# Two matmuls instead of three per block: the source's high and low part side by side in one 512-column matmul

## The chip, the core and the metric

The kernel runs on one core of a Trainium2 chip. The metric is device time in microseconds of one launch, the median of several runs. Beside the timed runs there is one execution with the hardware profiler; its span runs from the first to the last instruction.

## What is computed

A trunk of two transformer layers on 256 tokens with 1024 features, all in float32. Each layer is: half an FFN, an attention mixer, cross attention to 256 memory tokens, half an FFN. The mixer of the first layer joins differential and stick-breaking heads, that of the second is latent attention.

```python
def swiglu(h, w_gate, w_up, w_down):
    return (jax.nn.silu(h @ w_gate) * (h @ w_up)) @ w_down
...
    for layer in range(DEPTH):
        x = x + 0.5 * swiglu(rms_norm(x, ffn_norm[layer, 0]), ...)
        h = rms_norm(x, mix_norm[layer])
        x = x + mixer(h)            # ends in mixed @ w_out (layer 0), from_heads(o) @ w_o (layer 1)
        x = x + memory_cross_attention(rms_norm(x, xm_norm[layer]), rms_norm(mem, ...), ...)
        x = x + 0.5 * swiglu(rms_norm(x, ffn_norm[layer, 1]), ...)
```

The change concerns `@ w_down` (four times) and the output projections of the two mixers and the two cross attentions.

## The kernel before, in words

**Products from high and low parts.** Every operand of a large product is split into a high part (rounded to the matmul's type) and a low part, what the rounding left. A product of two such pairs is three matmuls: high x high, high x low, low x high (`mm3`, lines 268 to 272). Weights come from memory in chunks of up to 2048 columns. ACT casts a piece to `wh` (line 237), DVE subtracts to get `wl` (line 239); in attention phases GpSimd (POOL) takes the last 512 columns. Three buffers of `wh` and `wl` hold the chunks in flight, and SP's queue issues their transfers two chunks ahead.

**Layout.** The residual `x` lies feature-major, eight tiles of [128 features, 256 tokens]. In the down and output projections the weight block [128, 128] is the stationary operand and the source [128, 256 tokens] the moving one, so the result of an output tile needs 256 columns of a PSUM bank of 512. The sources (`slotr` in the trace) are slots of 512 columns; a slot holds two row blocks side by side, and high and low parts have slots of their own (`rpair`, line 469).

**FFN.** `ffn` makes 11 gate and 11 up products of two row blocks each and keeps the 22 split results in slots. Then `dp` runs over four pairs of output tiles; each pair takes two of the three `mm` banks, and for each of three weight chunks both tiles accumulate 8, 8 and 6 row blocks: 44 blocks a pair. PE's order is the program's.

**Output projections.** `out_g` does the same in the attention phases: 8 row blocks per tile after a mixer, 4 after cross attention. The first three tiles run as a group over the sources as they come, the other five one by one. There PE's order comes from a planner (`run`) that counts estimated times (`spend`, `drop`) and is fixed before the run. The order of the other engines' instructions is settled by the framework's scheduler.

**End of a tile.** `finish_dt` (line 481) adds the bank to `x` on DVE (line 484), splits the result times the next norm's gain into `xh` on ACT (line 462) and `xl` on DVE (line 463), squares it on ACT (line 496) and adds the squares on POOL (line 504). The next phase's first product reads the eight `xh`, `xl` pairs in turn, three matmuls each, and starts before the norm is known; the norm's sum and its spread over the partitions (line 526) are put in later.

Of the kernel before, what the change touches and what calls it, by code (L numbers as in the profile page):

```python
# [19 lines left out]
P = 128  # L20
# [10 lines left out]
# columns of the packed per-partition vectors  # L31
# [26 lines left out]
# estimates that settle the order of the tensor engine's work in the attention phases  # L58
# [92 lines left out]
def trunk_kernel(ctx, tc, wflat, xT_d, memT_d, gains_d, rows_d, cst_d, out_d):  # L151
# [35 lines left out]

    def alr():
        return alloc("r")
# [54 lines left out]
    def issue_part(i, h, n):  # L244
        """one of n parts of a chunk"""
# [21 lines left out]

    def mm3(out, a, b, first, last, **kw):
# [17 lines left out]
    # the tensor engine's clock rises while it works  # L286
# [10 lines left out]
    # chunk mask as a rank-one product: rows 0 and 64 hold it, the others are 0  # L297
# [15 lines left out]
    def setup():  # L313
# [12 lines left out]
        # rotary tables with the gains folded in  # L326
# [21 lines left out]
        # -(lambda) on every partition  # L348
# [69 lines left out]
    def run(first, tasks):  # L418
        """first: the first weight used"""
# [31 lines left out]
    def colsum(items, get):  # L451
        """items: lists of [128, 128] blocks; sums over partitions (and the list), tokens on partitions."""
# [7 lines left out]
    def split(hi, lo, src, g):  # L460
        """hi + lo = src * g (per partition)"""
# [7 lines left out]
    def rpair():  # L469
        return alr(), alr()  # L470
# [1078 lines left out]
```

## Time and profile before

| | us |
|---|---|
| median of 3 runs | 1130.59 (1129.61 to 1134.78) |
| span of the execution with the profile | 1131.1 |
| PE (TensorE) busy | 1104.2 |
| DVE busy | 783.8 |
| ACT busy | 653.3 |
| POOL busy | 214.5 |

Matmuls are pipelined: the length of one in the trace covers its whole way, so their pace is read from one start to the next. Each matmul has a weight load of its own (PEld), which runs beside the matmul before it. The stages follow each other in the span: first FFN to about 205 us, first mixer to 344, cross attention to 386, two FFNs to 576 and 765, latent mixer to 898, cross attention to 939, last FFN to the end.

### The profile page before, as it was taken

The numbers are of one execution on the slowest core, as the hardware profiler recorded it, in microseconds if no ns is written. First come the engines' busy times: TensorE is split into PE (matmuls) and PEld (weight loads), VectorE is DVE, ScalarE is ACT, GpSimd is POOL, SyncE is SP. The second block draws the span as 40 slices with busy tenths as digits, with TensorE's granted clock in tenths as the row PEclk, the third lists the DMA queues.
The fourth block names the chain that finished last, engine by engine and source line by source line (L and its number), as shares of the span: only waits on it lengthen the run. The fifth ranks groups of instructions, "written<-read, shape, count | busy, mean of one in ns | idle before, by whom it ended". The sixth has DMA issues, their size and how long they took to land.

```text
span 1131.1 us, 23384 instructions
## 1 busy us (share of the span) xinstructions
PE 1104.2 (98%) x9042; PEld 1084.4 (96%) x9042; DVE 783.8 (69%) x1864; ACT 653.3 (58%) x1765; POOL 214.5 (19%) x232
## 2 busy tenths in 40 slices
PE   7999999899999999999999999999979999999998
PEld 7999999899999999999999999999868999999998
DVE  6977656668876867676666767556688668676753
ACT  5755545677755755555555555556866566555542
POOL 4200001547244200000100000015861412000000
PEclk8999999999999999999999999999999999999999
DMA  6555555543445354545455555565342434555561
GB/s 232 218 192 183 180 193 187 187 150 119 143 150 174 114 188 169 192 175 200 170 186 189 185 187 178 176 197 187 113 131 66 153 134 147 203 182 192 177 207 65
DMA packets 49647, 191.39 MB, mean 169 GB/s; under 512 B 5632, under 2 KB 7296, under 8 KB 34432
## 3 DMA queue, kind: packets, MB, share of 16 engines
q1 hardware_dynamic: 49536, 189.89, 49.0%
q8 instruction: 71, 1.16, 0.4%
q14 instruction: 40, 0.33, 0.1%
HBM read 188.82 MB, written 1.05 MB: 168 GB/s over the span
## 4 chain that ended last, share of the span: by engine, by line
PE 85%; DVE 8%; issue 2%; ACT 2%; POOL 2%; DMA 0%; SPq 0%; DVEq 0%; POOLq 0%; ACTq 0%
PE mm L269 27%; PE mm L270 27%; PE mm L271 27%; DVE wl L239 3%; DVE xl L463 2%; PE t L723 1%; POOL sm L448 1%; ACT wh L237 1%; PE t L456 1%; DVE x L484 1%; POOL sl L448 0%; PE s L861 0%; PE o L1432 0%; PE s L1399 0%; ACT xh L462 0%
## 5 line engine op out<-in xcount | busy, mean ns | idle before, releaser
L237 ACT CAST wh<-wr 128x256 fp32r<-128x256 f32 (+1 forms) x1216 | 439.9, 433 | 341.8 <-PE mm L270 298.7
L239 DVE TENSOR_TENSOR wl<-wr,wh 128x256 fp32r<-128x256 f32 (+1 forms) x1171 | 482.6, 470 | 119.1 <-ACT wh L237 114.2
L270 PE MATMUL mm<-xl,wh 128*128 128x256 f32 x1584 | 447.7, 283 | 7.0 <-DVE xl L463 7.0
L269 PE MATMUL mm<-xh,wh 128*128 128x256 f32 x1584 | 448.7, 283 | 2.6 <-ACT wh L255 1.3
L271 PE MATMUL mm<-xh,wl 128*128 128x256 f32 x1584 | 446.4, 282 | 0.0
L270 PEld LDWEIGHTS mm<-xl,wh 128*128 128x128 f32 x1584 | 300.4, 190 | 9.3 <-DVE xl L463 9.1
L269 PEld LDWEIGHTS mm<-xh,wh 128*128 128x128 f32 x1584 | 300.5, 190 | 3.7 <-ACT wh L255 1.5
L271 PEld LDWEIGHTS mm<-xh,wl 128*128 128x128 f32 x1584 | 300.5, 190 | 0.2 <-DVE wl L256 0.2
L269 PE MATMUL mm<-slotr,wh 128*128 128x256 f32 x896 | 252.4, 282 | 0.0
L270 PE MATMUL mm<-slotr,wh 128*128 128x256 f32 x896 | 251.4, 281 | 0.0
L271 PE MATMUL mm<-slotr,wl 128*128 128x256 f32 x896 | 251.4, 281 | 0.0
L269 PEld LDWEIGHTS mm<-slotr,wh 128*128 128x128 f32 x896 | 168.9, 189 | 0.4 <-issue 0.3
L270 PEld LDWEIGHTS mm<-slotr,wh 128*128 128x128 f32 x896 | 168.9, 189 | 0.1
L271 PEld LDWEIGHTS mm<-slotr,wl 128*128 128x128 f32 x896 | 168.9, 188 | 0.0
L504 POOL TENSOR_TENSOR acc<-acc,sq 128x256 f32<-128x256 f32 x56 | 46.7, 833 | 529.5 <-ACT sq L496 523.8
L239 POOL TENSOR_TENSOR wl<-wr,wh 128x512 fp32r<-128x512 f32 x45 | 68.0, 1511 | 108.5 <-ACT wh L237 108.4
L671 DVE TENSOR_TENSOR slotf<-mm,rb 128x512 f32<-128x512 f32 x44 | 30.4, 690 | 79.1 <-PE mm L271 79.1
L663 DVE TENSOR_TENSOR slotf<-mm,rb 128x512 f32<-128x512 f32 x44 | 30.4, 690 | 37.4 <-PE mm L271 37.4
L269 PE MATMUL mm<-wh,slotr 128*128 128x256 f32 (+2 forms) x176 | 55.4, 315 | 0.0
L462 ACT ACTIVATE xh<-x,gains 128x256 fp32r<-128x256 f32 x64 | 32.0, 507 | 37.7 <-DVE x L484 35.2
L271 PE MATMUL mm<-wh,slotr 128*128 128x256 f32 (+2 forms) x176 | 53.3, 303 | 0.0
L270 PE MATMUL mm<-wl,slotr 128*128 128x256 f32 (+2 forms) x176 | 53.1, 302 | 0.0
(191 smaller groups left out, 1106.4 us busy)
## 6 DMA issues: line engine op xcount, KB each, us to landing
wr<-wflat SPq DMA_DIRECT2D x118, 1024.0 KB, 4.8
wr<-wflat SPq DMA_DIRECT2D x180, 256.0 KB, 4.0
wr<-wflat SPq DMA_DIRECT2D x16, 768.0 KB, 4.3
slotf<-memT SPq DMA_DIRECT2D x8, 256.0 KB, 6.0
x<-xT SPq DMA_DIRECT2D x4, 256.0 KB, 5.3
wr<-wflat SPq DMA_DIRECT2D x2, 512.0 KB, 8.1
out<-x SPq DMA_DIRECT2D x8, 128.0 KB, 3.7
cst<-cst SPq DMA_DIRECT2D x1, 256.0 KB, 8.1
```

What stands on the lines that cost most here:

```text
L237: A.copy(hi[:, a:b], raw[:, a:b])
L239: e.tensor_tensor(out=lo[:, a:b], in0=raw[:, a:b], in1=hi[:, a:b].bitcast(F32), op=ALU.subtract)
L269: PE.matmul(out, a[0], b[0], start=first, stop=False, **kw)
L270: PE.matmul(out, a[0], b[1], start=False, stop=False, **kw)
L271: PE.matmul(out, a[1], b[0], start=False, stop=last, **kw)
L448: G.tensor_tensor(out=y, in0=v, in1=mhalf[:, 0:n], op=ALU.pow)
L456: PE.matmul(ps[:, 2 * c:2 * c + 2], b, ones[:, 0:2], start=k == 0, stop=k == len(blocks) - 1)
L462: A.activation(hi, src, AF.Identity, scale=g)
L463: V.scalar_tensor_tensor(out=lo, in0=src, scalar=g, in1=hi.bitcast(F32), op0=ALU.mult, op1=ALU.subtract)
L504: G.tensor_tensor(out=st.acc, in0=st.acc, in1=sq, op=ALU.add)
L663: V.tensor_tensor(out=t.rearrange("p (a b) -> p a b", b=S), in0=pg.rearrange("p (a b) -> p a b", b=S), in1=rbb, op=ALU.mult)
L671: V.tensor_tensor(out=u.rearrange("p (a b) -> p a b", b=S), in0=pu.rearrange("p (a b) -> p a b", b=S), in1=rbb, op=ALU.mult)
```

## The change

Per block, `mm2` takes the place of `mm3` in the down and output projections. The source's high and low part now lie side by side in one slot of 1024 columns (`Pair`: two row blocks, each 256 columns high and 256 columns low). One matmul of 512 columns multiplies the high weights with both and fills the whole bank; one of 256 columns multiplies the low weights with the high part and accumulates onto the second half. `finish_dt` then adds the bank's two halves to `x` one after the other. Everything else that makes slots (memory tiles, latent pairs, stick-breaking sums) uses the same pairs and reads them in parts; the other products keep `mm3`. The planner counts 0.231 + 0.118 us for a block, and 1.2 for the release of a bank, instead of 0.327 and 0.8.

```diff
-            for key, n, dt in (("f", n32, F32), ("r", n32r, F32R)):
-                ar[key] = [pool.tile([P, 512], dt, name=nm("slot" + key)) for _ in range(n)]
+            for key, n, dt, w in (("f", n32, F32, 512), ("r", n32r // 2, F32R, 1024)):
+                ar[key] = [pool.tile([P, w], dt, name=nm("slot" + key)) for _ in range(n)]
...
+    def mm2(bank, w, src, first, last):
+        PE.matmul(bank[:, 0:512], w[0], src[2], start=first, stop=False)
+        PE.matmul(bank[:, S:512], w[1], src[0], start=False, stop=last)
+        spend(0.231 + 0.118)
...
-    def rpair():
-        return alr(), alr()
+    class Pair:
+        def __init__(self):
+            self.t = alloc("r")
+            self.v = self.t.rearrange("p (q h s) -> p q h s", h=2, s=S)
+            self.h, self.l = self.v[:, :, 0, :], self.v[:, :, 1, :]
+            self.blocks = [(self.v[:, q, 0, :], self.v[:, q, 1, :], self.t[:, q * 512:(q + 1) * 512])
+                           for q in range(2)]
...
     def finish_dt(dt, gc, ps=None, factor=1.0):
         xd = x[:, dt, :]
         if ps is not None:
-            V.scalar_tensor_tensor(out=xd, in0=ps, scalar=factor, in1=xd, op0=ALU.mult, op1=ALU.add)
+            for h in range(2):
+                V.scalar_tensor_tensor(out=xd, in0=ps[:, h * S:(h + 1) * S], scalar=factor, in1=xd,
+                                       op0=ALU.mult, op1=ALU.add)
...
     def out_g(keyf, nchunk, groups, gc):
...
-                mm3(pss[dt][:, 0:S], (w[0][:, k, j * P:(j + 1) * P], w[1][:, k, j * P:(j + 1) * P]),
+                mm2(pss[dt], (w[0][:, k, j * P:(j + 1) * P], w[1][:, k, j * P:(j + 1) * P]),
                     src[i], g == 0 and i == 0, g == len(groups) - 1 and i == len(rows_) - 1)
...
-                finish_dt(dt, gc, ps[:, 0:S])
-                drop(ps, 0.8)
+                finish_dt(dt, gc, ps)
+                drop(ps, 1.2)
...
     def ffn(l, j, gc, need_rb):
...
-            hh, hl = rpair()
-            split1(hh, hl, u)
+            h = Pair()
+            split1(h.h, h.l, u.rearrange("p (a b) -> p a b", b=S))
...
-                        mm3(pss[q][:, 0:S], (w[0][:, i, q * P:(q + 1) * P], w[1][:, i, q * P:(q + 1) * P]),
+                        mm2(pss[q], (w[0][:, i, q * P:(q + 1) * P], w[1][:, i, q * P:(q + 1) * P]),
                             hs[k], k == 0, k == FT - 1)
```

**PE, start of the first FFN's down projection.** Each row is a matmul: output bank, source slot and weight buffer, then the size of the output. Before:

```order
L269 MATMUL mm_1869<-slotr_109,wh_1727 128x256
L270 MATMUL mm_1869<-slotr_110,wh_1727 128x256
L271 MATMUL mm_1869<-slotr_109,wl_1726 128x256
L269 MATMUL mm_1869<-slotr_109,wh_1727 128x256
L270 MATMUL mm_1869<-slotr_110,wh_1727 128x256
L271 MATMUL mm_1869<-slotr_109,wl_1726 128x256
```

And now, the same two blocks and half of the next:

```order
L268 MATMUL mm_1858<-slotr_109,wh_1716 128x512
L269 MATMUL mm_1858<-slotr_109,wl_1715 128x256
L268 MATMUL mm_1858<-slotr_109,wh_1716 128x512
L269 MATMUL mm_1858<-slotr_109,wl_1715 128x256
L268 MATMUL mm_1858<-slotr_110,wh_1716 128x512
```

High and low part are in one slot, and a block has two rows. PE's order is the same in all else, but for two output blocks in the latent mixer that stand behind a group of four transposes instead of ahead of it.

**DVE, end of the first FFN** (tiles 6 and 7 of the last pair; `wl_...` is the next phase's weight chunk; line 496 of the changed kernel is the addition, 467 the low part, 236 the weight subtraction). Before:

```order
L484 SCALAR_TENSOR_TENSOR x<-mm_2486,x 128x256 [waits PE_49]
L463 SCALAR_TENSOR_TENSOR xl_2668<-x,gains,xh_2667 128x256 [waits Activation_49]
L484 SCALAR_TENSOR_TENSOR x<-mm_2487,x 128x256 [waits PE_49]
L239 TENSOR_TENSOR wl_2738<-wr_2737,wh_2739 128x512 [waits DMAHW2_49,Activation_49]
L239 TENSOR_TENSOR wl_2738<-wr_2737,wh_2739 128x512 [waits DMAHW3_49,Activation_49]
L463 SCALAR_TENSOR_TENSOR xl_2676<-x,gains,xh_2675 128x256 [waits Activation_49]
L239 TENSOR_TENSOR wl_2738<-wr_2737,wh_2739 128x512 [waits DMAHW4_49,Activation_49]
```

Now:

```order
L496 SCALAR_TENSOR_TENSOR x<-mm_2349,x 128x256 [waits PE_49]
L496 SCALAR_TENSOR_TENSOR x<-mm_2349,x 128x256 [waits DVE_49]
L467 SCALAR_TENSOR_TENSOR xl_2488<-x,gains,xh_2487 128x256 [waits Activation_49]
L496 SCALAR_TENSOR_TENSOR x<-mm_2350,x 128x256 [waits PE_49]
L236 TENSOR_TENSOR wl_2549<-wr_2548,wh_2550 128x512 [waits DMAHW2_49,Activation_49]
L496 SCALAR_TENSOR_TENSOR x<-mm_2350,x 128x256 [waits DVE_49]
L236 TENSOR_TENSOR wl_2549<-wr_2548,wh_2550 128x512 [waits DMAHW3_49,Activation_49]
L236 TENSOR_TENSOR wl_2549<-wr_2548,wh_2550 128x512 [waits DMAHW4_49,Activation_49]
L467 SCALAR_TENSOR_TENSOR xl_2497<-x,gains,xh_2496 128x256 [waits Activation_49]
```

A second addition, which waits for the first, and a third weight subtraction stand between tile 7's matmuls and its low part.

**DVE, end of the first cross attention** (tiles 4 to 7; the weight chunk is the next FFN's). Before:

```order
L463 SCALAR_TENSOR_TENSOR xl_4946<-x,gains,xh_4945 128x256 [waits Activation_49]
L484 SCALAR_TENSOR_TENSOR x<-mm_4952,x 128x256 [waits PE_49]
L484 SCALAR_TENSOR_TENSOR x<-mm_4973,x 128x256 [waits PE_49]
L463 SCALAR_TENSOR_TENSOR xl_4967<-x,gains,xh_4966 128x256 [waits Activation_49]
L484 SCALAR_TENSOR_TENSOR x<-mm_4994,x 128x256 [waits PE_49]
L463 SCALAR_TENSOR_TENSOR xl_4988<-x,gains,xh_4987 128x256 [waits Activation_49]
L239 TENSOR_TENSOR wl_5053<-wr_5052,wh_5054 128x256 [waits DMAHW0_49,Activation_49]
L463 SCALAR_TENSOR_TENSOR xl_5009<-x,gains,xh_5008 128x256 [waits Activation_49]
```

Now:

```order
L496 SCALAR_TENSOR_TENSOR x<-mm_4692,x 128x256 [waits PE_49]
L496 SCALAR_TENSOR_TENSOR x<-mm_4674,x 128x256 [waits DVE_49]
L496 SCALAR_TENSOR_TENSOR x<-mm_4692,x 128x256 [waits DVE_49]
L496 SCALAR_TENSOR_TENSOR x<-mm_4710,x 128x256 [waits PE_49]
L467 SCALAR_TENSOR_TENSOR xl_4686<-x,gains,xh_4685 128x256 [waits Activation_49]
L496 SCALAR_TENSOR_TENSOR x<-mm_4710,x 128x256 [waits DVE_49]
L467 SCALAR_TENSOR_TENSOR xl_4704<-x,gains,xh_4703 128x256 [waits Activation_49]
L496 SCALAR_TENSOR_TENSOR x<-mm_4728,x 128x256 [waits PE_49]
L467 SCALAR_TENSOR_TENSOR xl_4722<-x,gains,xh_4721 128x256 [waits Activation_49]
L496 SCALAR_TENSOR_TENSOR x<-mm_4728,x 128x256 [waits DVE_49]
L236 TENSOR_TENSOR wl_4773<-wr_4772,wh_4774 128x256 [waits DMAHW0_49]
L236 TENSOR_TENSOR wl_4773<-wr_4772,wh_4774 128x256 [waits Activation_49] x2
```

Behind these rows stands the last low part: three weight subtractions ahead of it instead of one. The chunk before (`wl_4655`, seven rows) now stands ahead of tile 4's first addition.

## Rows read from the trace of the kernel before

**Rows 1.** The page: busy time of the engines, the last chain's shares.
```profile
PE 1104.2 (98%) x9042; PEld 1084.4 (96%) x9042; DVE 783.8 (69%) x1864; ACT 653.3 (58%) x1765; POOL 214.5 (19%) x232
...
PE 85%; DVE 8%; issue 2%; ACT 2%; POOL 2%; DMA 0%; SPq 0%; DVEq 0%; POOLq 0%; ACTq 0%
PE mm L269 27%; PE mm L270 27%; PE mm L271 27%; DVE wl L239 3%; DVE xl L463 2%; PE t L723 1%; POOL sm L448 1%; ACT wh L237 1%; PE t L456 1%; DVE x L484 1%; POOL sl L448 0%; PE s L861 0%; PE o L1432 0%; PE s L1399 0%; ACT xh L462 0%
```

**Rows 2.** The page's groups: count, busy us, mean ns | idle before, releaser.
```profile
L269 PE MATMUL mm<-slotr,wh 128*128 128x256 f32 x896 | 252.4, 282 | 0.0
...
L484 DVE SCALAR_TENSOR_TENSOR x<-mm,x 128x256 f32<-128x256 f32 x64 | 26.6, 418 | 23.6 <-PE mm L271 23.6
```

**Rows 3.** Timeline, DVE, first down projection: start, length (us), instruction, [idle before].
```profile
156.74 0.42 DVE L484 SCALAR_TENSOR_TENSOR x<-mm,x 128x256 f32<-128x256 f32 x1
...
172.41 0.42 DVE L484 SCALAR_TENSOR_TENSOR x<-mm,x 128x256 f32<-128x256 f32 x1
```

**Rows 4.** Timeline, PE, latent mixer: 256 columns, then 512.
```profile
790.05 0.28 PE L269 MATMUL mm<-wh,slotr 128*128 128x256 f32 x1
...
791.85 0.28 PE L269 MATMUL mm<-wh,slotr 128*128 128x256 f32 x1
...
792.22 0.39 PE L269 MATMUL mm<-wh,slotr 128*128 128x512 f32 x1
792.45 0.39 PE L270 MATMUL mm<-wl,slotr 128*128 128x512 f32 x1
792.68 0.40 PE L271 MATMUL mm<-wh,slotr 128*128 128x512 f32 x1
792.92 0.39 PE L269 MATMUL mm<-wh,slotr 128*128 128x512 f32 x1
```

**Rows 5.** Timeline, PE, latent mixer: 384 columns, the first and the nineteenth.
```profile
809.78 0.34 PE L269 MATMUL mm<-wh,slotr 128*128 128x384 f32 x1
...
812.96 0.34 PE L269 MATMUL mm<-wh,slotr 128*128 128x384 f32 x1
```

**Rows 6.** Waits of PE: who waited <- for whom: us in total, times, longest.
```profile
PE mm L270 <- DVE xl L463: 7.0, 7, 1.4
PE t L526 <- issue: 2.9, 1, 2.9
```

**Rows 7.** Timeline, DVE and PE, ends of the first FFN and the second (last row).
```profile
204.95 0.42 DVE L484 SCALAR_TENSOR_TENSOR x<-mm,x 128x256 f32<-128x256 f32 x1 [0.36 <-PE mm L271]
205.53 1.29 DVE L239 TENSOR_TENSOR wl<-wr,wh 128x512 fp32r<-128x512 f32 x2 [0.15 <-ACT wh L237]
206.75 0.48 DVE L463 SCALAR_TENSOR_TENSOR xl<-x,gains,xh 128x256 fp32r<-128x256 f32 x1
...
207.37 0.31 PE L270 MATMUL mm<-xl,wh 128*128 128x256 f32 x1
...
219.60 0.76 PE L526 MATMUL t<-slotf,ones 128*128 128x256 f32 x2 [2.85 <-issue]
...
578.17 0.47 DVE L463 SCALAR_TENSOR_TENSOR xl<-x,gains,xh 128x256 fp32r<-128x256 f32 x1
```

**Rows 8.** Timeline, DVE and PE, start of the FFN after cross attention.
```profile
389.19 0.94 DVE L463 SCALAR_TENSOR_TENSOR xl<-x,gains,xh 128x256 fp32r<-128x256 f32 x1
...
390.19 0.38 PE L270 MATMUL mm<-xl,wh 128*128 128x256 f32 x1 [0.83 <-DVE xl L463]
```

**Rows 9.** Timeline, PE, start of cross attention; busy us by stretch before two boundaries.
```profile
348.33 0.38 PE L270 MATMUL mm<-xl,wh 128*128 128x256 f32 x1 [0.94 <-DVE xl L463]
...
331.00:346.00 15.00, 15.00 (x129) 15.00 (x128) 13.65 (x22) 10.86 (x26) 10.03 (x9) 1.00 0.44 141
379.00:391.00 12.00, 11.00 (x90) 10.61 (x90) 11.57 (x26) 10.14 (x31) 5.96 (x7) 1.00 0.40 148
```

The columns of the last two are: length; PE, PEld, DVE, ACT and POOL busy (and their instructions); granted clock, share of the DMA engines, GB/s.

**Rows 10.** Timeline, DVE and SP's queue, end of the run.
```profile
1128.01 0.42 DVE L484 SCALAR_TENSOR_TENSOR x<-mm,x 128x256 f32<-128x256 f32 x1 [1.69 <-PE mm L271]
1128.46 0.33 SPq L486 DMA_DIRECT2D out<-x  x1
```

More of the change, by code (lines that the diff above doesn't have):

```diff
@@ L594, in tm_g @@
             for k in range(KT):
-                a = tuple(z[:, t * P:(t + 1) * P] for z in xg[k])
+                a = tuple(z[:, t * P:(t + 1) * P] for z in xg[k][:2])
                 mm3(ps[:, t * S:(t + 1) * S], a, (w[0][:, k, :], w[1][:, k, :]), k == 0, k == KT - 1)
@@ L673, in ffn @@
             V.tensor_tensor(out=u, in0=u, in1=s, op=ALU.mult)
-            hh, hl = rpair()
-            split1(hh, hl, u)
+            h = Pair()
+            split1(h.h, h.l, u.rearrange("p (a b) -> p a b", b=S))
             rel(u, s)
-            tiles += [hh, hl]
-            for q in range(2):
-                hs.append((hh[:, q * S:(q + 1) * S], hl[:, q * S:(q + 1) * S]))
+            tiles.append(h.t)
+            hs += h.blocks
         begin_phase()
@@ L742, in mem_gain @@
             nc.sync.dma_start(raw.rearrange("p (a b) -> p a b", b=S), memT_d[:, 2 * q:2 * q + 2, :])
-            h, lo = rpair()
-            memstate["tiles"] = memstate.get("tiles", []) + [h, lo]
+            h = Pair()
+            memstate["tiles"] = memstate.get("tiles", []) + [h.t]
             for j in range(2):
-                sl_ = slice(j * S, (j + 1) * S)
-                split(h[:, sl_], lo[:, sl_], raw[:, sl_], gcol(G_MEM + l * KT + 2 * q + j))
-                xm.append((h[:, sl_], lo[:, sl_]))
+                split(h.blocks[j][0], h.blocks[j][1], raw[:, j * S:(j + 1) * S], gcol(G_MEM + l * KT + 2 * q + j))
+            xm += h.blocks
             if first:
@@ L883, in attend @@
             rel(*pT)
-            hh, hl = rpair()
-            split1(hh, hl, po)
-            tiles.extend([hh, hl])
-            srcs[hp] += [(hh[:, j * S:(j + 1) * S], hl[:, j * S:(j + 1) * S]) for j in range(2)]
+            h = Pair()
+            split1(h.h, h.l, po.rearrange("p (a b) -> p a b", b=S))
+            tiles.append(h.t)
+            srcs[hp] += h.blocks
             drop(po, 1.3)
@@ L920, in mixer_ab, with add_src @@
         raw = {}
-        def add_src(i, hh, hl):
-            tiles.extend([hh, hl])
-            srcs[i] += [(hh[:, j * S:(j + 1) * S], hl[:, j * S:(j + 1) * S]) for j in range(2)]
+        def add_src(i, h):
+            tiles.append(h.t)
+            srcs[i] += h.blocks
         def products():
@@ L1028, in stick @@
                 rel(e)
-                hh, hl = rpair()
-                split1(hh[:, 0:384], hl[:, 0:384], sp[:, 0:384])
-                sps.append((sp, hh, hl))
-            for i, (z, (sp, hh, hl)) in enumerate(zip(zs, sps)):
+                pr = Pair().t
+                split1(pr[:, 0:384], pr[:, 512:896], sp[:, 0:384])
+                sps.append((sp, pr))
+            for i, (z, (sp, pr)) in enumerate(zip(zs, sps)):
                 yield dict(lat=EST_AB['st2'] if i else EST_AB['st1'])
-                for h_ in (hh, hl):
-                    PE.matmul(z[:, 0:384], ntri, h_[:, 0:384], start=False, stop=False, skip_group_check=True)
+                for o in (0, 512):
+                    PE.matmul(z[:, 0:384], ntri, pr[:, o:o + 384], start=False, stop=False, skip_group_check=True)
                 PE.matmul(z[:, P:S], nones, sp[:, S:384], start=False, stop=True, skip_group_check=True)
@@ L1156, in turn_o @@
             pt = transpose4([oa[t][:, (2 * g + j) * P:(2 * g + j + 1) * P] for j in range(2) for t in range(2)])
-            hh, hl = rpair()
-            split(hh, hl, pt, gsub)
-            add_src(2 + g, hh, hl)
+            h = Pair()
+            split(h.h, h.l, pt.rearrange("p (a b) -> p a b", b=S), gsub)
+            add_src(2 + g, h)
             drop(pt, 1.4)
@@ L1180, in latent @@
             pairs, sqs = lat[key]
-            hh, hl = rpair()
+            h = Pair()
             for j in range(2):
-                sl_ = slice(j * S, (j + 1) * S)
-                split(hh[:, sl_], hl[:, sl_], ps[:, sl_], gcol(gc0 + j))
-                pairs.append((hh[:, sl_], hl[:, sl_]))
-            lat_tiles.extend([hh, hl])
+                split(h.blocks[j][0], h.blocks[j][1], ps[:, j * S:(j + 1) * S], gcol(gc0 + j))
+            pairs += h.blocks
+            lat_tiles.append(h.t)
             sq = al()
@@ L1436, in attend @@
             rel(*pT)
-            hh, hl = rpair()
-            split1(hh, hl, po)
-            tiles.extend([hh, hl])
-            srcs[n] += [(hh[:, j * S:(j + 1) * S], hl[:, j * S:(j + 1) * S]) for j in range(2)]
+            h = Pair()
+            split1(h.h, h.l, po.rearrange("p (a b) -> p a b", b=S))
+            tiles.append(h.t)
+            srcs[n] += h.blocks
             drop(po, 1.3)
```

16 lines of the change are left out of this document (7 added, 9 removed).

## The prediction

> **What bounds the kernel now.** I read the page first: TensorE is busy for 98% of the span, and the chain that ended last lies on it for 85%, 81% in the three lines of the three-matmul helper [rows 1]. So a shorter stream of matmuls shortens the time wherever the engine does not wait. Of that stream the change touches the 896 blocks that write an output tile from a slot: 704 in the four down projections (4 x 8 tiles x 22 row blocks), 192 in the four output projections [rows 2].
>
> The length of one matmul in the trace (281 ns) holds its way through the array; what counts is start to start. The DVE's additions give it without any counting of matmuls: between the first additions of two neighbouring pairs of tiles lie 2 x 22 x 3 = 132 matmuls, and they are 172.41 - 156.74 = 15.67 us apart, 118.7 ns each [rows 3]. TensorE's granted clock is 1.00 in the stretches that I read [rows 9], so 2.4 GHz, at which 256 columns alone are 106.7 ns. Something is on top, and how it divides between "per matmul" and "per column" is all that this change can win.
>
> The trace of before has wide matmuls, in the key and value products of the latent mixer, right behind narrow ones of the same kind. Fifteen of 256 columns take 791.85 - 790.05 = 1.80 us, 120.0 ns each; three of 512 take 792.92 - 792.22 = 0.70 us, 233.3 ns each [rows 4]. Eighteen of 384 take 3.18 us, 176.7 ns [rows 5]. The three widths lie on one line: 6.7 ns per matmul and 0.443 ns per column (384 x 0.443 + 6.7 = 176.7). Two narrow ones in one wide one thus save 6.7 ns.
>
> Then I read the waits: PE lost 7.0 us in seven waits for the low part of the normed residual, and 2.9 us in one wait of the matmul that spreads the norm [rows 6]. The seven lie at the start and at the ends of stages, where the last addition, the high part and the low part follow each other and the next stage's eighth block needs the result. That is the place where this change adds work.
>
> **The change part by part.** *Matmuls.* Per block three of 256 columns become one of 512 and one of 256. In the 704 down blocks that is 704 x 6.7 ns, **-4.7 us**, all on the path, since PE does not wait inside the down stages. The 192 blocks of the output projections would give 1.3 us more, but these end behind the DVE (below), so I count 0 there. Bounds for all 896: nothing, if a wide one follows the slowest distance of the wide rows (0.24 us, two narrow ones are 0.237), and 6.6 us at the fastest distance (0.23 us, 7.4 ns a block). I stay with the mean of three. A loss is unlikely, since that mean is below two narrow ones in the same row.
>
> *Weight loads.* One in three goes. No PE wait on them stands inside the down stages, so 0.
>
> *A second addition per tile.* 64 more of 0.42 us on DVE [rows 2], and the order shows that each waits for the DVE's own first addition. Inside a stage this is covered: a pair of tiles takes 15.67 us and the additions 0.84 more; the third bank and the 22 blocks ahead of the next need cover the later release. At a stage's end it is not. Start of the first addition: the wide matmul of the last block ends one narrow matmul earlier, 0.12 us gained.
>
> *End of the run.* The last addition starts at 1128.01 and the output's transfer is issued at 1128.46 [rows 10]. One more addition, 0.42, with some 0.05 for the wait, less 0.12: **+0.35**.
>
> *FFN into an attention stage* (twice). Before, two weight subtractions (1.29 together) stand between the last addition and the low part, which is ready at 206.75 + 0.48 = 207.23; the matmul that reads it starts at 207.37 without a wait [rows 7], so the slack is 0.1 at most. In the new order the second addition (0.42) and a third subtraction (0.65) stand there too: 1.07 later, less 0.12 and the slack, a wait of some 0.85. At the first of the two PE soon waits 2.85 us for the norm's spread [rows 7], which hangs on the DVE's work on freshly loaded memory tiles, not on PE; the new wait disappears in it: 0. At the second, into the latent mixer, no such wait follows within 30 us: **+0.9**. Bounds 0 and 1.0 for each.
>
> *Mixer into cross attention* (twice). PE already waits 0.94 us for the low part, and the DVE is busy 13.65 of the 15 us before [rows 9]. Five tiles finish there one by one: five additions are 2.1 us against 1.35 us of idle time. Bounds: 0.35 (own addition only) and 2.1 (none of the idle time is usable, since it is spent waiting for casts). I take 1.0: the overflow of 0.75 and a little of the idle time. **+2.0**.
>
> *Cross attention into FFN* (twice). PE waits 0.83 us [rows 8], the DVE is busy 11.57 of 12 us [rows 9]. Bounds 0.35 and 2.1 - 0.43 = 1.7. I take 0.6, towards the lower end: in the new order seven weight subtractions stand ahead of the fifth tile's addition, so that the tail holds additions, low parts and three subtractions, where before the low part was itself stretched to 0.94 us beside them. **+1.2**.
>
> *FFN into FFN* (once): the low part starts at 578.17 [rows 7] and PE does not wait. A third subtraction and the second addition move it, but the first low part of the pair is moved too. 0 to 0.6, **+0.2**.
>
> *The rest.* The casts and subtractions into slots write two strided halves, same count and elements; 0. The larger slots are handed out in the same turn. The planner's new figures move two output blocks in the latent mixer past one group of transposes: 0.
>
> Sum: -4.7 + 0.35 + 0.9 + 2.0 + 1.2 + 0.2 = **-0.05 us**. The execution with the profile had a span of 1131.1 us; the median of the three runs lies 0.5 us below it. 1131.1 - 0.05 - 0.5 = 1130.6 us (rounded).
>
> **The rivals.** *The ends are covered* (0.20). If the stage ends cost their lower bounds (0 + 0 + 0.7 + 0.7 + 0 + 0.35 = 1.75) and the output projections keep their gain (6.7 ns x 896 = 6.0), the sum is -4.25: 1126.4. For it: the low part at the cross boundary was stretched by other work, which can fall elsewhere. Against it: the DVE has hardly any idle time there [rows 9].
>
> *The DVE becomes the bound at the ends of the output projections* (0.13), slower than before. One mechanism: five late tiles x one addition, none of the idle time usable: 2 x 2.1 + 2 x 1.7 = 7.6 instead of 3.2, so +4.35: 1135.0. It decides from the point where these additions delay the low part by over 0.8 us at each of the four boundaries; with the 1.45 us of the other ends the matmuls' 4.7 us are eaten then. For it speaks that DVE waits in order, so an addition that waits for PE holds the subtractions behind it.
>
> *The overhead goes with the columns* (0.15), so the wide matmul is worth two narrow ones and the change wins nothing on PE. For it: one of three wide ones took 0.24 us to the next (792.68 to 792.92), two narrow ones 0.24 [rows 4]; and the three widths were read in another stage, where the moving operand is a weight. Against it: all three widths fit one line. The ends alone would give +4.65: 1135.2 us, and half of the saving 1132.9.
>
> The Trainium skill speaks for a part of this: TensorE: Matmul & The Clock Gate, "Back-to-back issue gap", gives the distance of warm matmuls as N / 2.4 ns plus about 2.5 ns. The trace disagrees, with 118.7 and 233.3 ns where that would be 109 and 216. By that split the down blocks would save 1.8 us, and the time would come to 1133.5 us.
>
> **How the numbers follow.** My case, gain and ends cancel, has 0.52, with its own range of 1128 to 1133. About 0.5% (5.65 us) is what a measurement of this kernel can tell from no change. Faster by more (under 1124.9) needs the covered ends and the highest gain: 0.05. Slower by more (over 1136.2) needs the DVE case or that of the columns with the upper bounds of the other ends: 0.09. Same: 0.86. The range of 8 in 10 reaches from the lower part of the covered case to the DVE case, 1125.5 to 1135.5.
>
> **What would show it.** Right: first additions of neighbouring pairs 15.67 - 44 x 0.0067 = 15.37 us apart in the first FFN; wide matmuls 231 to 233 ns apart from the next; at the boundary into the latent mixer a new PE wait of near 0.9 us for the low part, at the first boundary the same with a shorter wait of the norm's spread; waits near 2 us into cross attention and 1.4 us into the FFN. Wrong: pairs still 15.67 us apart (no gain); PE waits for the low part that do not grow (covered), or that pass 2.5 us (DVE bound).

## The result and the profile after

The changed kernel takes 1146.11 us (median; 1143.56 to 1147.07), the kernel before 1132.68 us on the same chip: ratio 1.0097, 95% interval 1.0073 to 1.012. It is slower by about 1%, and 10.6 us above the upper end of the range. The profiled execution has a span of 1141.8 us (1131.1 before).

The page of the changed kernel, busy time of the engines, the last chain's shares, the group of the wide matmuls and that of the additions (count | busy us, mean ns | idle before, releaser), against [rows 1, 2]:

```profile
PE 1103.9 (97%) x8146; PEld 1043.9 (91%) x8146; DVE 806.9 (71%) x1928; ACT 653.5 (57%) x1765; POOL 208.8 (18%) x232
...
PE 82%; DVE 9%; issue 3%; POOL 3%; ACT 3%; DMA 0%; SPq 0%; DVEq 0%; POOLq 0%; ACTq 0%
...
L268 PE MATMUL mm<-slotr,wh 128*128 128x512 f32 x896 | 312.5, 393 | 5.4 <-DVE x L496 5.4
...
L496 DVE SCALAR_TENSOR_TENSOR x<-mm,x 128x256 f32<-128x256 f32 x128 | 52.2, 419 | 22.6 <-PE mm L269 21.7
```

The chain's share of PE fell from 85% to 82%, DVE's rose from 8% to 9%, and a wide matmul now waits for the addition, which no matmul of the projections did for long before. The waits of PE, longest first (who waited <- for whom: us in total, times, longest), against [rows 6]:

```profile
PE mm L274 <- DVE xl L467: 10.0, 8, 2.0
PE mm L268 <- DVE x L496: 5.4, 2, 2.7
PE mm L273 <- ACT xh L466: 4.2, 4, 1.2
```

7.0 us of waits for the low part have become 10.0, and two new kinds are there: 5.4 us for a bank that the additions have not yet released, 4.2 us for the high part.

The best reading is by stretches. I take the first and the last matmul of each of the eight residual projections from PE's timeline and compare the lengths of the projections and of what lies between them. Each cell is the difference to the profile of before, in us ("again" is a second profile of the same kernel; the other columns are experiments below).

| stretch | before again | after | after again | one add | mm3, two adds | adds adjacent | short add | best |
|---|---|---|---|---|---|---|---|---|
| 4 down projections (249.5) | -1.4 | -5.9 | -5.9 | -5.9 | -1.4 | -5.9 | -5.9 | -4.9 |
| 2 mixers' output projections (49.3) | 0.0 | -0.9 | -0.9 | -0.9 | 0.0 | +1.0 | -0.9 | 0.0 |
| 2 from there to cross's projection (60.1) | 0.0 | +8.8 | +6.2 | +0.8 | +8.5 | +13.4 | +0.6 | -1.8 |
| 2 cross's output projections (22.9) | 0.0 | +5.3 | +6.7 | -0.6 | +6.5 | +1.1 | +2.6 | 0.0 |
| 2 from cross to the FFN's down (254.3) | -1.3 | +0.1 | +0.2 | -1.8 | 0.0 | +1.1 | -3.5 | -1.3 |
| first FFN to the mixer's projection (116.3) | -0.1 | -0.5 | -0.6 | -0.8 | +1.6 | +1.9 | +0.1 | +0.9 |
| FFN to the next FFN's down (126.3) | -1.3 | +1.2 | -0.2 | -0.6 | -0.8 | -0.5 | -0.3 | -0.1 |
| FFN to the latent mixer's projection (106.9) | +1.3 | +2.6 | +4.6 | +1.1 | +1.4 | +1.6 | +1.2 | +1.3 |
| start to the first down (142.1) | -0.1 | -0.5 | -1.1 | 0.0 | -1.0 | -0.9 | -1.0 | +0.3 |
| end (3.4) | 0.0 | +0.5 | +0.5 | +0.1 | +0.5 | +0.5 | +0.3 | 0.0 |
| sum | -2.9 | +10.7 | +9.6 | -8.6 | +15.4 | +13.2 | -6.7 | -5.5 |

The matmuls paid what they should: 5.9 us in the down projections, 4.5 against the second profile of the kernel before. The loss is 14 us at the output projections: 8.8 between a mixer's projection and cross attention's, 5.3 inside the latter. (Differences of 1.3 to 1.4 in the stretches with an FFN's gate and up products, and of 0.7 in a down projection of three matmuls, are chance, and 1.1 to 1.4 in the stretch from an FFN to the latent mixer's projection go with the clock; the last section shows both.)

Three places, read in the trace. **Mixer into cross attention.** DVE's timeline at the end of the first mixer (start, length, instruction, [idle before]); the additions x1 and x2 are tiles 6 and 7:

```profile
341.82 0.41 DVE L496 SCALAR_TENSOR_TENSOR x<-mm,x 128x256 f32<-128x256 f32 x1
342.15 1.51 DVE L236 TENSOR_TENSOR wl<-wr,wh 128x512 fp32r<-128x512 f32 x1
343.59 0.41 DVE L496 SCALAR_TENSOR_TENSOR x<-mm,x 128x256 f32<-128x256 f32 x1
344.58 0.48 DVE L467 SCALAR_TENSOR_TENSOR xl<-x,gains,xh 128x256 fp32r<-128x256 f32 x1 [0.58 <-ACT xh L466]
344.98 0.88 DVE L496 SCALAR_TENSOR_TENSOR x<-mm,x 128x256 f32<-128x256 f32 x2
...
346.97 0.48 DVE L467 SCALAR_TENSOR_TENSOR xl<-x,gains,xh 128x256 fp32r<-128x256 f32 x1
```

PE's timeline beside it: the last matmul of the projection, then the next stage's waits.

```profile
341.34 0.28 PE L269 MATMUL mm<-slotr,wl 128*128 128x256 f32 x1
...
344.60 0.38 PE L273 MATMUL mm<-xh,wh 128*128 128x256 f32 x1 [0.86 <-ACT xh L466]
...
346.86 0.38 PE L273 MATMUL mm<-xh,wh 128*128 128x256 f32 x1 [1.24 <-ACT xh L466]
347.51 0.39 PE L274 MATMUL mm<-xl,wh 128*128 128x256 f32 x1 [0.26 <-DVE xl L467]
```

Tile 7's matmuls end at 341.34 + 0.28 = 341.6, its first addition starts 3.4 us later. DVE is late with both last tiles, and PE now waits for the high parts of two tiles, where it waited once for a low part (0.94, [rows 9]). After that the granted clock falls. Busy us by stretch, as in [rows 9] (length, PE, PEld, DVE, ACT, POOL, granted clock, DMA, GB/s):

```profile
348.00:350.00 2.00, 2.00 (x15) 2.00 (x14) 0.59 (x1) 0.00 (x0) 1.73 (x2) 0.71 0.27 100
350.00:352.00 2.00, 2.00 (x12) 2.00 (x11) 0.00 (x0) 0.00 (x0) 0.00 (x0) 0.50 0.39 114
...
354.00:356.00 2.00, 2.00 (x20) 2.00 (x19) 1.29 (x2) 1.45 (x3) 0.47 (x1) 1.00 0.29 112
```

At 0.50 (1.2 GHz) 12 matmuls lie wholly or in part in 2 us, at 1.00 (2.4 GHz) 20. Some 16 of them start 213 ns apart instead of 118, which is 1.5 us of the 3.9 that this boundary cost.

**Cross attention's projection**, DVE's timeline:

```profile
384.30 2.64 DVE L236 TENSOR_TENSOR wl<-wr,wh 128x256 fp32r<-128x256 f32 x6
386.86 1.74 DVE L496 SCALAR_TENSOR_TENSOR x<-mm,x 128x256 f32<-128x256 f32 x5
```

And PE's:

```profile
388.08 0.47 PE L268 MATMUL mm<-slotr,wh 128*128 128x512 f32 x1 [2.68 <-DVE x L496]
```

Six weight subtractions stand ahead of five additions, all three banks are full, and PE waits 2.68 us. **FFN into mixer** (first FFN), DVE's timeline, against [rows 7]:

```profile
202.94 0.42 DVE L496 SCALAR_TENSOR_TENSOR x<-mm,x 128x256 f32<-128x256 f32 x1
203.43 0.82 DVE L236 TENSOR_TENSOR wl<-wr,wh 128x512 fp32r<-128x512 f32 x1
204.17 0.41 DVE L496 SCALAR_TENSOR_TENSOR x<-mm,x 128x256 f32<-128x256 f32 x1
204.50 2.35 DVE L236 TENSOR_TENSOR wl<-wr,wh 128x512 fp32r<-128x512 f32 x2
206.78 0.94 DVE L467 SCALAR_TENSOR_TENSOR xl<-x,gains,xh 128x256 fp32r<-128x256 f32 x1
```

The matmul on PE that waits for this low part:

```profile
207.78 0.39 PE L274 MATMUL mm<-xl,wh 128*128 128x256 f32 x1 [1.97 <-DVE xl L467]
```

Two subtractions that took 1.29 us together now take 2.35 and the low part 0.94 instead of 0.48. POOL's timeline has it at work at the same moments:

```profile
205.04 1.27 POOL L236 TENSOR_TENSOR wl<-wr,wh 128x512 fp32r<-128x512 f32 x1 [1.33 <-ACT wh L234]
206.27 1.17 POOL L517 TENSOR_TENSOR acc<-acc,sq 128x256 f32<-128x256 f32 x1
```

### The profile page after: what moved, and what is told of

It is laid out like the page before. It is cut to its first block, busy times and chain, and to the rows that moved or that the text cites. A ratio compares the mean times of both kernels' runs of the same rounds, so it can differ in the third digit from the quotient of the medians.

```text
span 1141.8 us, 21678 instructions
## 1 busy us (share of the span) xinstructions
PE 1103.9 (97%) x8146; PEld 1043.9 (91%) x8146; DVE 806.9 (71%) x1928; ACT 653.5 (57%) x1765; POOL 208.8 (18%) x232
## 4 chain that ended last, share of the span: by engine, by line
PE 82%; DVE 9%; issue 3%; POOL 3%; ACT 3%; DMA 0%; SPq 0%; DVEq 0%; POOLq 0%; ACTq 0%
PE mm L274 18%; PE mm L273 18%; PE mm L275 18%; PE mm L268 15%; PE mm L269 8%; DVE wl L236 4%; DVE xl L467 1%; ACT wh L234 1%; DVE x L496 1%; PE t L735 1%; POOL sm L452 1%; POOL acc L517 1%; PE t L460 1%; POOL sl L452 0%; PE s L872 0%
## 5 line engine op out<-in xcount | busy, mean ns | idle before, releaser
L268 PE MATMUL mm<-slotr,wh 128*128 128x512 f32 x896 | 312.5, 393 | 5.4 <-DVE x L496 5.4
L268 PEld LDWEIGHTS mm<-slotr,wh 128*128 128x128 f32 x896 | 168.2, 188 | 42.9 <-issue 6.3
L236 POOL TENSOR_TENSOR wl<-wr,wh 128x512 fp32r<-128x512 f32 x45 | 65.5, 1455 | 107.2 <-ACT wh L234 107.1
L496 DVE SCALAR_TENSOR_TENSOR x<-mm,x 128x256 f32<-128x256 f32 x128 | 52.2, 419 | 22.6 <-PE mm L269 21.7
L467 DVE SCALAR_TENSOR_TENSOR xl<-x,gains,xh 128x256 fp32r<-128x256 f32 x64 | 43.5, 684 | 6.5 <-ACT xh L466 6.4
```

What stands on the lines that cost most here:

```text
L236: e.tensor_tensor(out=lo[:, a:b], in0=raw[:, a:b], in1=hi[:, a:b].bitcast(F32), op=ALU.subtract)
L268: PE.matmul(bank[:, 0:512], w[0], src[2], start=first, stop=False)
L467: V.scalar_tensor_tensor(out=lo, in0=src, scalar=g, in1=hi.bitcast(F32), op0=ALU.mult, op1=ALU.subtract)
L496: V.scalar_tensor_tensor(out=xd, in0=ps[:, h * S:(h + 1) * S], scalar=factor, in1=xd, op0=ALU.mult, op1=ALU.add)
```

## The experiments

Theory A: the second addition costs all of the loss, by its own time and by the order of DVE's work that comes with it. Rival B: something else of the change does (the shorter stream of matmuls, the paired slots, the planner's figures). Four kernels part them. The kernels of this section ran on several chips, on which the kernel before took 1132.2 to 1134.9 us (medians). Each ratio is to the kernel before on the same chip, so kernels are best compared by their ratios.

**One addition per tile.**

```diff
-            for h in range(2):
-                V.scalar_tensor_tensor(out=xd, in0=ps[:, h * S:(h + 1) * S], ...)
+            V.scalar_tensor_tensor(out=xd, in0=ps[:, 0:S], scalar=factor, in1=xd, ...)
```

> The changed kernel with only the first of the two additions per tile; left out is the product of the high weights and the source's low part, with the low weights' product, which lie in the bank's second half. Matmuls, slots and the planner's figures stay. Theory A (the second addition, by its own time and by the order of DVE's work that it brings, costs about 18 us at the stage ends, and the matmuls give some 7): near 1125.5 us, blocks of the down projections 346 ns apart, no wait of PE for the addition in the cross projections. Rival B (the shorter stream of matmuls, the paired slots or the planner's figures cost it: weights come no faster, so PE waits for them instead): 1138 us or more.

Measured: 1126.89 us, ratio 0.9942 (0.9916 to 0.9968). The loss is gone, the gain of the matmuls stands (table, "one add"). B falls.

**Three matmuls and two additions** (kernel before):

```diff
-            V.scalar_tensor_tensor(out=xd, in0=ps, scalar=factor, in1=xd, ...)
+            for f_ in (factor, 0.0):
+                V.scalar_tensor_tensor(out=xd, in0=ps, scalar=f_, in1=xd, ...)
```

> The kernel before with a second addition per tile, of zero times the same bank, behind the first; three matmuls per block as before. Theory A: 1132.7 plus 13 to 19, so 1146 to 1152 us, with PE waiting for banks in the cross projections. Rival B: within 3 us of 1132.7.

Measured: 1149.18 us, ratio 1.0162 (1.0133 to 1.019), with +8.5 us into cross attention and +6.5 inside its projections: the changed kernel's loss without its matmuls.

**The change in the down projections alone, and in the output projections alone.**

```diff
 out_g:  -  mm2(pss[dt], ...)            finish_dt(dt, gc, ps)
         +  mm3(pss[dt][:, 0:S], ...)    finish_dt(dt, gc, ps[:, 0:S])
```

> Two matmuls per block and two additions per tile in the down projections alone; the output projections with three matmuls and one addition. Theory A: the down blocks give 5.9 us, the FFN's ends take back 3 to 5 (from the changed kernel's trace: -0.5, +1.2, +2.6, +0.5), so 1129 to 1132 us. Rival B: the loss goes with the faster down stage, 1138 us or more.

Measured: 1132.09 us, ratio 0.9996 (0.9978 to 1.0014).

```diff
 ffn:    -  mm2(pss[q], ...)             finish_dt(dp * 2 + q, gc, pss[q], 0.5)
         +  mm3(pss[q][:, 0:S], ...)     finish_dt(dp * 2 + q, gc, pss[q][:, 0:S], 0.5)
```

> Two matmuls and two additions in the output projections alone; the down projections as before. Theory A: +2.6 in each cross projection, +3.9 and +4.9 from the mixers into cross attention, about 0 from there into the FFN, -0.9 for the mixers' own blocks: near 1146 us. Rival B: within 2 us of 1132.7.

Measured: 1147.25 us, ratio 1.0136 (1.0113 to 1.0159). The output projections make the whole loss; in the FFNs gain and ends cancel.

**Is it the order, or DVE's time?** In the next kernel the order of DVE's additions, low parts and weight subtractions is held to that of the one-addition kernel, with each second addition right behind its first.

```diff
+    chain = [...]   # additions, low parts, weight subtractions in the one-addition kernel's order
+    for a_, b_ in zip(chain, chain[1:]):
+        tc.add_manual_dep(b_.ins, a_.ins.name, ...NoSync..., reason="order")
```

> The changed kernel, whole, with DVE's additions, low parts and weight subtractions held in the order that the kernel with one addition per tile has, and each second addition right behind its first. Theory A1 (most of the loss is the order: weight subtractions that moved between the additions and ahead of the low parts): 0.4 to 0.5 us per late addition remains, about 8 us over the one-addition kernel's 1126.9, so 1131 to 1137 us. Theory A2 (the additions' own time on a full DVE is the loss, whatever the order): 1143 to 1149 us.

Measured: 1145.86 us, ratio 1.0104 (1.0083 to 1.0126): no better. The order decides where the loss falls, not how much it is: 4.2 us less inside cross attention's projections (the six subtractions no longer stand ahead of the additions), 4.6 more on the way into them and 1.9 more inside the mixers' own. I had expected the order to be most of it; that was wrong.

**A second addition of 32 columns.**

```diff
-            for h in range(2):
-                V.scalar_tensor_tensor(out=xd, in0=ps[:, h * S:(h + 1) * S], ...)
+            for h, n in ((0, S), (1, 32)):
+                V.scalar_tensor_tensor(out=xd[:, 0:n], in0=ps[:, h * S:h * S + n], ...)
```

> The changed kernel with the second addition cut from 256 columns to 32; left out is the rest of the second half's sum. The instruction, its place behind the first and its wait stay, its time goes from 0.42 us to some 0.1 to 0.2. If the loss is DVE's time: about a third of the 19 us between one addition (1126.9) and two (1146) remains, 1130 to 1135 us. If it is the chain of instructions and waits, whatever their length: 1141 us or more.

Measured: 1129.53 us, ratio 0.9957 (0.9934 to 0.9979). The page has the short one at 186 ns (64 of them, 11.8 us), the full one at 418. 0.23 us less for each of 64 additions, 15 us of DVE, takes 1.4% or 16 us off the time (ratio 1.0097 to 0.9957). In the profiles some 4 us of that is the clock: it falls behind the mixers' waits in the changed kernel's first profile and stays at 1.00 there in this one. At the mixer's end the short and the adjacent kernel have the very same order on DVE, so their timelines can be laid side by side. Short, tiles 4 to 6 (x2 is a tile's two additions):

```profile
336.00 0.64 DVE L496 SCALAR_TENSOR_TENSOR x<-mm,x 128x256 f32<-128x256 f32 x2
337.21 0.49 DVE L467 SCALAR_TENSOR_TENSOR xl<-x,gains,xh 128x256 fp32r<-128x256 f32 x1 [0.58 <-ACT xh L466]
...
339.45 0.96 DVE L467 SCALAR_TENSOR_TENSOR xl<-x,gains,xh 128x256 fp32r<-128x256 f32 x1
...
340.94 0.63 DVE L496 SCALAR_TENSOR_TENSOR x<-mm,x 128x256 f32<-128x256 f32 x2
```

Full, adjacent, the same tiles:

```profile
340.56 0.87 DVE L509 SCALAR_TENSOR_TENSOR x<-mm,x 128x256 f32<-128x256 f32 x2
342.56 1.21 DVE L479 SCALAR_TENSOR_TENSOR xl<-x,gains,xh 128x256 fp32r<-128x256 f32 x1 [1.14 <-ACT xh L478]
...
345.69 0.97 DVE L479 SCALAR_TENSOR_TENSOR xl<-x,gains,xh 128x256 fp32r<-128x256 f32 x1
...
347.18 0.87 DVE L509 SCALAR_TENSOR_TENSOR x<-mm,x 128x256 f32<-128x256 f32 x2
```

Two tiles are one turn of DVE's work: 340.94 - 336.00 = 4.94 us with the short addition, 347.18 - 340.56 = 6.62 with the full one. TensorE needs 16 blocks at 346.7 ns = 5.55 us for the same two tiles. In the kernel before the turn is 344.10 - 339.40 = 4.70 us, against 16 x 356 ns = 5.70 on TensorE. Its additions to tiles 4, 6 and 7, and the last matmuls of tiles 4 and 7:

```profile
339.40 0.41 DVE L484 SCALAR_TENSOR_TENSOR x<-mm,x 128x256 f32<-128x256 f32 x1
...
344.10 0.41 DVE L484 SCALAR_TENSOR_TENSOR x<-mm,x 128x256 f32<-128x256 f32 x1
...
345.54 0.41 DVE L484 SCALAR_TENSOR_TENSOR x<-mm,x 128x256 f32<-128x256 f32 x1
```

```profile
335.96 0.28 PE L271 MATMUL mm<-slotr,wl 128*128 128x256 f32 x1
...
344.51 0.28 PE L271 MATMUL mm<-slotr,wl 128*128 128x256 f32 x1
```

So there was 1.0 us to spare in this turn, and two second additions of 0.46 with the shorter matmuls' 0.15 use it up: 4.70 + 0.92 = 5.62 against 5.55. From there on DVE is the slower of the two, its instructions meet others' (the low part at 1.21 us, and 1.14 us of waiting for a high part that stands behind casts on ACT), and the turn grows to 6.62. At the second mixer's end the turns are 4.71 us (before), 4.92 (short) and 7.62 (full).

The spare time was not idle in the kernel before either. DVE came late into these turns there too: the addition to tile 4 started 3.2 us behind the end of the tile's last matmul (335.96 + 0.28 = 336.24), that to tile 7 only 0.8 us behind (344.79). DVE caught up 2.4 us in three tiles. With the short addition it still does (from 2.6 us behind to 0.8), with the full one hardly (from 5.3 to 4.5), and the next stage pays for what is left.

**A longer way without DVE's time.** The second addition also lengthens the way from addition to high part to low part; this kernel does that on ACT.

```diff
+        if ps is not None:
+            A.activation(h, xd, AF.Identity, scale=gcol(gc + dt))
         split(h, l, xd, gcol(gc + dt))
```

> The kernel with one addition per tile, whose high part is made twice by ACT (the same values, written over), so that the way from a tile's addition to its low part grows by some 0.4 to 0.5 us, as with a second addition, but by ACT's time and not by DVE's. The second halves of the banks are left out, as there. If the longer way (addition, high part, low part, and the casts queued behind it on ACT) is the loss: near 1140 us or more. If it is the 0.42 us of DVE's own time per tile: 2 to 5 us over the 1126.9 of one addition, 1129 to 1132 us.

Measured: 1132.65 us, ratio 0.9991 (0.9977 to 1.0005) against 0.9942 for the one-addition kernel, 0.5% or 5.5 us more and a little above what I gave for "DVE's own time". The way grew by more than planned, since ACT's square of the tile came to stand between the two high parts: they start 0.72 us apart (337.80 and 338.52, first mixer). The stretches between its projections differ from those of that kernel by -0.9 to +2.5 us, the projections themselves not at all. The longer way is at most a third of the loss (0.5% of the 1.55% between one addition and two); the rest takes DVE's time.

**What is left of the change.** Second additions only where DVE has room: the first three pairs of tiles in each down projection.

```diff
-                        mm2(pss[q], ...)
+                        (mm2 if dp < 3 else mm3)(pss[q] if dp < 3 else pss[q][:, 0:S], ...)
```

> Two matmuls per block and two additions per tile in the first three pairs of tiles of each down projection; the last pair of each, and the output projections, with three matmuls and one addition. Theory A (only the second additions at a stage's end cost): three quarters of the down projections' 5.9 us are won and nothing is paid, 1132.2 - 4.4 = 1127.8 us. Rival (second additions cost inside a stage as well, where DVE and the banks cover them): 1131 us or more.

Measured: 1129.98 us, ratio 0.9966 (0.9951 to 0.9981). The time lies between the two figures, but the kernel before took 1134.92 us on this chip, and 0.34% of that is 3.9 us of the 4.4: theory A.

Then the last low part ahead of the two weight subtractions at five stage ends, by the same chain of order as above:

```diff
 DVE's order at an FFN's end (A addition, L low part, W weight subtraction):
-A L A W W L W W
+A L A L W W W W
```

> As the kernel with the last pair in three matmuls, but at five stage ends (the three FFNs that are followed by a stage with a low part, but for the last, and both mixers) DVE makes the last low part ahead of the two weight subtractions that stood before it. If the low part is what PE waits for: 0.9 us less at the two mixers' ends, some 0.5 elsewhere, so 1 to 3 us below the kernel without this order. Rival (the subtractions' weights are wanted just as soon): no difference, or up to 2 us slower.

Measured: 1128.22 us, ratio 0.9949 (0.9931 to 0.9966). The mixers' ends give 0.94 and 0.95 us in the trace; the time alone doesn't show it, since the interval overlaps that of the kernel without this order.

The same order with three matmuls and one addition throughout:

```diff
-                        (mm2 if dp < 3 else mm3)(pss[q] if dp < 3 else pss[q][:, 0:S], ...)
+                        mm3(pss[q][:, 0:S], ...)
```

> Three matmuls and one addition everywhere (paired slots kept), with the last low part ahead of two weight subtractions at five stage ends. It parts the two gains of the kernel at 1128.2 us: if the two matmuls in the first three pairs give their 4.4 us, this one lies at 1131 to 1133 us, 2 us under the kernel before and 3 to 5 above that one; if the order alone did it, at 1128.

Measured: 1132.33 us, ratio 0.9987 (0.9972 to 1.0002): the order alone is worth 0.1%, which is not clear of nothing; the rest is the two matmuls.

And the low part first at the ends of both cross attentions too:

```diff
-L A A L A L W L W
+L A A L A L L W W
```

> As the kernel at 1128.2 us, with the low part first at the ends of both cross attentions too, ahead of one weight subtraction. PE waits 0.8 us there for it: 0.4 to 0.6 us less at each, 1127.2 us. Rival (the weights are wanted as soon): 1128 or more.

Measured: 1126.13 us, ratio 0.9929 (0.9908 to 0.9951), the fastest of the kernels that leave nothing out, and faster than the kernel before and the changed one. Its interval overlaps that of the kernel without this last step (0.9949), so the step itself is not shown by the time. PE's waits around the first cross attention's end, of before and then of this kernel:

```profile
PE mm L270 <- DVE xl L463: 0.8, 1, 0.8
PE mm L269 <- DVE x L484: 0.2, 1, 0.2
```

```profile
PE mm L285 <- DVE x L509: 0.7, 1, 0.7
```

The wait for the low part is gone there; one for an addition, 0.7 where it was 0.2, takes part of its place.

**Both kernels profiled once more**, to see what is the program's and what is chance:

> The kernel before, profiled once more. The mean distance of 256-column matmuls was 118.7 ns in three of its four stretches of gate and up products and 117.3 in the last. If that is set by the program: the same four values. If it falls out anew in each execution: another pattern of the two values, and 1.4 us of time with each.

> The changed kernel, profiled once more. What the ends of the mixers (+3.9 and +4.9 us) and the cross projections (+2.6 each) cost should come back to 0.3 us, if they are the program's; the distance of 118.7 or 117.3 ns per stretch and the 1.3 us of the latent mixer's start may differ, if they fall out anew in each execution.

Measured: 1129.95 and 1142.56 us. Columns "again" of the table: the down and the mixers' projections come back, and so does the wait for a bank inside cross attention's (2.68 us in all four). The distances of matmuls do not, the second mixer's end cost 2.4 us instead of 4.9, and cross attention's projections 3.3 and 3.4 instead of 2.6 each. The last two differences are the clock. At the second mixer's end TensorE waits 0.89 and 1.24 us for two high parts in the first profile, 0.89 and 1.25 in the second. Then the granted clock fell in the first and not in the second, where the same work is some 2 us later in the span (changed kernel, then changed kernel again, the stretch with the second wait and the one behind it):

```profile
905.00:907.00 2.00, 1.24 (x4) 0.95 (x5) 2.00 (x4) 1.45 (x4) 0.91 (x2) 0.55 0.96 338
907.00:909.00 2.00, 2.00 (x11) 2.00 (x11) 0.41 (x1) 0.00 (x0) 1.55 (x1) 0.50 0.14 52
```

```profile
907.00:909.00 2.00, 1.11 (x7) 0.92 (x8) 2.00 (x4) 1.39 (x4) 0.98 (x2) 1.00 0.95 347
909.00:911.00 2.00, 2.00 (x20) 2.00 (x19) 0.35 (x1) 0.00 (x0) 1.50 (x1) 1.00 0.07 27
```

In cross attention it is the other way round: behind the wait for a bank the granted clock is 1.00 in the first profile (388 to 390 us) and 0.50 in the second. So a mixer's end costs 2.4 us where the clock holds; the kernel with the change in the output projections alone shows the same 2.4 at its second mixer, without a fall. Falls add 1.5 us (first mixer, both profiles) and 2.5 (second mixer, first profile).

## Why the prediction was wrong, step by step

- **Down matmuls, -4.7.** Right in kind, and the size lies between -5.9 (first profile of before) and -4.5 (second). A block now takes 346.7 ns in every down projection. In the kernel before it took 356.0 in three and 352.0 in the last, the second time 356.0 in one and 352.0 in three, so the gain depends on which of two distances the kernel before falls into (last section). That the figure came out so near is in part luck. The 6.7 ns came from wide matmuls that follow each other (233.3 ns) behind narrow ones 120.0 ns apart; between narrow ones the wide one takes 229.2 ns (mean of PE's start distances in the first down projection). By the split that the Trainium skill gives for an isolated matmul (TensorE: Matmul & The Clock Gate, "Back-to-back issue gap", quoted in the prediction) a block would be 325 ns; the trace does not agree. That section says itself that a stream with a weight load for each matmul keeps another distance, which the prediction left out.
- **Output projections' matmuls, 0.** They do gain: 0.9 in the mixers, 0.6 in cross attention where the additions don't hold them up (one addition).
- **Ends of FFNs, +0.35, 0, +0.9, +0.2.** End of the run +0.5. The first FFN's end as told: the new wait (1.97 us) took the place of that of the norm's spread, 2.85 before and none now. Into the latent mixer the wait is 1.97 us, not 0.9: I added up instructions at the lengths that they had, and they grew beside POOL. (The stretch as a whole is longer by 2.6 and 4.6; the 2.0 between the two go with falls of the granted clock in the second profile alone, to 0.54 and 0.60 at 770 to 774 us, behind the same wait, and once more at 849.) FFN into FFN: a new wait of 0.9 us, and +1.2 in the stretch.
- **Mixer into cross attention, 2 x 1.0.** This is the step that failed first: 3.9 and 4.9, in the second profile 3.8 and 2.4. My upper bound was five additions' own time, 2.1 us, and I took less than half of it, since DVE had 1.35 us of idle time there. But that time was what DVE caught up in. It takes its work in order, and where its turn is longer than TensorE's, lateness is handed from tile to tile, and weights and high parts behind it are late too: 2.4 us, a little over the bound, where the clock holds. The other 1.5 to 2.5 us is the fall of the granted clock behind these waits, a term that the prediction did not have.
- **Cross attention into FFN, 2 x 0.6.** The second step that failed: about 0 there; the loss lies ahead of it, 2.6 us inside each projection, where PE waits 2.68 for a bank. The prediction let the third bank cover a later release inside a stage. It did so in the down projections (15 us a pair of tiles) and not here. The order shown ahead of the prediction had the seven subtractions in front of tile 4's addition; I read from it what is late for the next stage and not that three banks hold up the same stage. Together the four boundaries were put at 3.2 us and cost 14.1 (12.9 in the second profile).
- **The rivals.** "DVE becomes the bound" was the right mechanism, at 0.13 and at 1135.0 us, 11 us short. Its idle time had been read as a reserve (1.35 of 15 us); the reserve that counted was 1.0 us in the last turn of two tiles, and the change needed 1.07. "The overhead goes with the columns" fell, and so did "the ends are covered".
- **What would show it.** Pairs 15.37 us apart: they are 171.24 - 155.99 = 15.25, which is 44 blocks of 346.7 ns. Waits for the low part "that pass 2.5 us (DVE bound)": they did not, the longest is 2.0; the bound showed as waits for banks and high parts instead.

```profile
155.99 0.87 DVE L496 SCALAR_TENSOR_TENSOR x<-mm,x 128x256 f32<-128x256 f32 x2
...
171.24 0.88 DVE L496 SCALAR_TENSOR_TENSOR x<-mm,x 128x256 f32<-128x256 f32 x2
```

## What to carry to other kernels

When a change moves work from a busy engine to another, compare the other's turn per tile with the busy engine's time for the same tile, stage by stage: second additions of 0.42 us were free in the down projections (15 us a pair) and cost some 14 us at the output projections, where two tiles took DVE 4.7 us of TensorE's 5.7 and the rest served to catch up. Their own time is no upper bound there: five late additions are 2.1 us, a mixer's end cost 2.4 where the clock held and up to 4.9 where it fell behind the waits. And such a change can be kept where the room is: with two matmuls in three pairs of tiles of four, and the low part ahead of work that can wait, the kernel is 0.7% faster than before.

## What the runs showed of the hardware

**Two distances for the same matmuls.** A stretch of 256-column matmuls runs at 117.3 or at 118.7 ns start to start (once at 120.0), for a whole stage, and which one falls out anew in each execution: the kernel before had 118.7, 118.7, 118.7, 117.3 in its four gate and up stages, and 118.7, 117.3, 117.3, 117.3 the second time. The evacuations of the up products in the third FFN show it, 96 matmuls apart (before, then before again):

```profile
L671 DVE TENSOR_TENSOR slotf<-mm,rb x7: 691/692/692, 611.8 to 680.1; 128x512 f32<-128x512 f32 x7
```

```profile
L671 DVE TENSOR_TENSOR slotf<-mm,rb x8: 691/692/693, 609.3 to 688.1; 128x512 f32<-128x512 f32 x8
```

(680.1 - 611.8) / 6 = 11.38 us and (688.1 - 609.3) / 7 = 11.26: 118.6 and 117.3 ns for each of 96. It is worth 1.3 to 1.4 us a stage, so several us of the spread of a kernel's times may be this; what sets it is open. The pairs of a wide and a narrow matmul had one distance, 346.7 ns, in all seven profiles (of six kernels) that have them in every tile of the down projections.

**The clock is not the same in each execution.** The stretch from an FFN to the latent mixer's projection took 1.3 us more in the second profile of the kernel before. In that one alone the granted clock was at 0.50 for 3.4 us at 824 and again at 841 us, where TensorE stands idle for part of the time (before, then before again):

```profile
823.00:828.00 5.00, 2.94 (x24) 2.61 (x22) 2.79 (x9) 1.52 (x4) 4.03 (x7) 1.00 0.58 175
```

```profile
823.00:828.00 5.00, 3.75 (x15) 3.31 (x16) 3.54 (x6) 1.91 (x4) 4.84 (x4) 0.66 0.41 128
```

The one-addition, the short-addition and the best kernel show two such falls there and +1.1 to +1.3 us, the kernel with the low part first at five ends none and 0.0. Why the clock falls behind the same waits in one execution and not in another is open.

**DVE beside POOL.** The low part takes 0.48 us, and about twice that if an instruction of POOL had begun before it (medians over the kernel before: 945 ns of 29, which range from 521 to 1307; 478 ns of the 27 where POOL began later, 475 of the 8 alone). In 28 of the 29 it ends 0.28 to 0.29 us behind the end of POOL's instruction, however long that is. The additions, with one operand in PSUM, take 0.41 to 0.42 in all three cases. One of each, before, end of the first mixer:

```profile
342.55 0.75 POOL L504 TENSOR_TENSOR acc<-acc,sq 128x256 f32<-128x256 f32 x1 [1.01 <-ACT sq L496]
...
342.62 0.96 DVE L463 SCALAR_TENSOR_TENSOR xl<-x,gains,xh 128x256 fp32r<-128x256 f32 x1
```

The Trainium skill states it (SBUF — State Buffer, "SBUF: two separate sides"): the port pair that DVE and GpSimd share is an exclusive lock, and whoever starts first, GpSimd or an instruction of DVE with two inputs in SBUF, holds it for the whole instruction. The trace agrees, in the additions with their operand in PSUM too. It means that the lengths of DVE's instructions at a stage's end can't be carried over from before, since a shift by some tenths of a microsecond decides who meets whom.
